# A gated top-2 dispatch: without the early two-row store, the first group of 65 rows in five stores of 13

## The chip, the cores and the metric

One core of a Trainium2 chip runs the kernel. The metric is the device time in microseconds. The kernel before takes 239.43 us, the median of three runs (239.3 to 239.44).

## What is computed

For each of 16 x 1024 tokens the kernel takes a vector of 512 float32 numbers and 8 router logits. It finds the two largest probabilities of the softmax, normalises them to sum 1, and writes the vector twice, once scaled by each.

```python
probs = np.exp(router_logits - logits_max)
probs = probs / np.sum(probs, axis=-1, keepdims=True)
topk_indices = np.argsort(probs, axis=-1)[..., -k:]
topk_probs = np.take_along_axis(probs, topk_indices, axis=-1)
topk_probs = topk_probs / np.sum(topk_probs, axis=-1, keepdims=True)
x_expanded = x[:, :, np.newaxis, :].repeat(k, axis=2)
return (x_expanded * topk_probs[..., np.newaxis]).astype(np.float32)
```

So `x`, 33.6 MB, is read once, and the output, 67.1 MB, is written once. The two weights depend only on the difference of the two largest logits: a sigmoid of it and a sigmoid of its negative.

## The kernel before

The 16384 tokens stand as 128 partitions of 128 rows. They are worked in two groups (`GROUPS`, L16), of 65 and of 63 rows on each partition. A "row" below is one row on all 128 partitions: 256 KB of `x`, or 512 KB of output, since each vector is written twice.

Two buffers in on-chip memory hold everything. `xs` has room for 65 rows of `x`, `osp` for 18 rows of output (L97, L98). A third, small tile, `WA`, holds the weights of all rows. The logits and the intermediate results of the weight calculation lie at the end of `osp` (L101, L102), so that no store can be written there before the weights are known.

For each group a loop issues the loads of `LOADS` on SyncE's queue (L112). After the first load of 6 rows it also issues two loads of logits (L105, L106), and VectorE and ScalarE work out the weights (L53 to L68). Then a second loop goes through `STORES` (L119). An entry names the number of rows, the home of the output, the number of rows that ScalarE multiplies rather than VectorE, and the queue that issues the store. The multiplication is one VectorE instruction for all its rows (L127), and two ScalarE instructions for each row of ScalarE's (L135). The store follows (L138).

The home of an output is either `osp` or `xs` itself. In `xs` a block of n output rows takes the place of 2n rows of `x` that have been multiplied already or are just being multiplied: output row i is written to rows a + 2i and a + 2i + 1, not ahead of the row that is read. The homes alternate, so that one can be filled while the other is being stored.

In the first group the loads have 6, 28 and 31 rows, and the stores 2, 16, 16, 16 and 15. The store of 2 rows needs only the first load; ScalarE's queue (q10 in the profile) issues it. All other transfers are issued by SyncE, in the order of the program, on one queue (q1): the three loads, four stores of group 0, two loads of group 1, four stores of group 1. A waiting instruction on SyncE holds up all that follow it there. The loads of group 1 go into the rows of `xs` that group 0's outputs occupy, and wait for those stores.

Of the kernel before, what the change touches and what calls it, by code (L numbers as in the profile page):

```python
# [1 line left out]

# [4 lines left out]

F32 = mybir.dt.float32
ALU = mybir.AluOpType
ACTF = mybir.ActivationFunctionType  # L10
P = 128
E = 8
D = 512


GROUPS = [65, 63]  # L16
M = sum(GROUPS)


LOADS = [[6, 28, 31], [32, 31]]  # L20


STORES = [
    [
        (2, ("osp", 0), 0, "ACT"),
        (16, ("osp", 2), 0, "SP"),
        (16, ("x", 2), 0, "SP"),
        (16, ("osp", 0), 4, "SP"),
        (15, ("x", 35), 0, "SP"),
    ],  # L30
    [
        (16, ("osp", 0), 1, "SP"),
        (16, ("x", 0), 0, "SP"),
        (16, ("osp", 0), 4, "SP"),
        (15, ("x", 33), 0, "SP"),
    ],
]
OSP = 18


def top2_weights(nc, scratch, logits, WA):

    used = [0]

    def cut(n):
        a = scratch[:, used[0] : used[0] + M * n].rearrange("p (m n) -> p m n", n=n)
        used[0] += M * n
        return a

    a, b = logits[:, :, 0:4], logits[:, :, 4:8]  # L50
    hi = cut(4)
    lo = b
    nc.vector.tensor_tensor(hi, a, b, op=ALU.max)  # L53
    nc.vector.tensor_tensor(lo, a, b, op=ALU.min)  # L54
    n = 4
    while n > 1:
        n //= 2
        a, b = hi[:, :, 0:n], hi[:, :, n : 2 * n]
        nhi, nlo, tmp = cut(n), cut(n), cut(n)
        nc.vector.tensor_tensor(tmp, lo[:, :, 0:n], lo[:, :, n : 2 * n], op=ALU.max)  # L60
        nc.vector.tensor_tensor(nlo, a, b, op=ALU.min)  # L61
        nc.vector.tensor_tensor(nlo, nlo, tmp, op=ALU.max)  # L62
        nc.vector.tensor_tensor(nhi, a, b, op=ALU.max)  # L63
        hi, lo = nhi, nlo
    dlt = cut(1)
    nc.vector.tensor_tensor(dlt, hi, lo, op=ALU.subtract)  # L66
    nc.scalar.activation(WA[:, :, 0], dlt[:, :, 0], ACTF.Sigmoid, scale=-1.0)  # L67
    nc.scalar.activation(WA[:, :, 1], dlt[:, :, 0], ACTF.Sigmoid, scale=1.0)  # L68


@with_exitstack
def kernel(
    ctx: ExitStack,
    tc: tile.TileContext,
    x: bass.AP,
    router_logits: bass.AP,
    k: bass.AP,
    out: bass.AP,
):
    nc = tc.nc  # L80
    N = x.shape[0] * x.shape[1]
    assert int(k) == 2 and router_logits.shape[-1] == E and x.shape[2] == D
    assert N == P * M
    xf = x.rearrange("b s d -> (b s) d")
    of = out.rearrange("b s k d -> (b s) k d")
    rf = router_logits.rearrange("b s e -> (b s) e")
    x_v, o_v, rl_v = [], [], []
    t0 = 0
    for n in GROUPS:
        t1 = t0 + P * n  # L90
        x_v.append(xf[t0:t1].rearrange("(p m) d -> p m d", p=P))
        o_v.append(of[t0:t1].rearrange("(p m) k d -> p m k d", p=P))
        rl_v.append(rf[t0:t1].rearrange("(p m) e -> p m e", p=P))
        t0 = t1

    pool = ctx.enter_context(tc.tile_pool(name="pool", bufs=1))
    xs = pool.tile([P, max(GROUPS), D], F32)  # L97
    osp = pool.tile([P, OSP, 2, D], F32)  # L98
    WA = pool.tile([P, M, 2], F32)

    logits = osp[:, OSP - 1].rearrange("p k d -> p (k d)").rearrange("p (m e) -> p m e", e=E)  # L101
    scratch = osp[:, OSP - 3 : OSP - 1].rearrange("p r k d -> p (r k d)")  # L102

    def load_logits():
        nc.sync.dma_start(logits[:, : GROUPS[0]], rl_v[0])  # L105
        nc.sync.dma_start(logits[:, GROUPS[0] :], rl_v[1])  # L106

    m0 = 0
    for g, G in enumerate(GROUPS):
        r = 0  # L110
        for n in LOADS[g]:
            nc.sync.dma_start(xs[:, r : r + n, :], x_v[g][:, r : r + n, :])  # L112
            if g == 0 and r < 6 <= r + n:
                load_logits()
                top2_weights(nc, scratch, logits, WA)
            r += n
        assert r == G
        r = 0
        for n, (home, a), by_act, queue in STORES[g]:  # L119
            if home == "x":  # L120
                og = xs[:, a : a + 2 * n, :].rearrange("p (r k) d -> p r k d", k=2)
            else:
                og = osp[:, a : a + n]
            v = n - by_act
            w = WA[:, m0 + r : m0 + r + n, :]
            if v:
                nc.vector.tensor_tensor(  # L127
                    og[:, :v],
                    xs[:, r : r + v, :].unsqueeze(2).to_broadcast([P, v, 2, D]),
                    w[:, :v].unsqueeze(3).to_broadcast([P, v, 2, D]),  # L130
                    op=ALU.mult,
                )
            for i in range(v, n):
                for c in range(2):
                    nc.scalar.activation(  # L135
                        og[:, i, c], xs[:, r + i, :], ACTF.Copy, scale=w[:, i, c : c + 1]
                    )
            {"SP": nc.sync, "ACT": nc.scalar}[queue].dma_start(o_v[g][:, r : r + n], og)  # L138
            r += n
        assert r == G  # L140
        m0 += G


# [1 line left out]
_INS = ['x', 'router_logits', 'k']  # L145
_OUTS = [((16, 1024, 2, 512), 'float32')]

_NUMBERS = {'k': 2}


# [26 lines left out]
```

## Time and profile before

| | |
|---|---|
| median of three runs | 239.43 us |
| the profiled execution's own time | 239.38 us |
| its span | 237.6 us |
| VectorE busy | 132.2 us |
| ScalarE busy | 13.2 us |
| moved, read and written | 34.08 MB and 67.11 MB |
| mean rate over the span | 426 GB/s |

The span runs from the first to the last event in the trace; the execution's own time holds a little more at both ends. A transfer's time to landing counts from its issue until its completion is signalled, and so includes the time that it stands in the queue behind others. In the tables of groups, a line gives the source line, the engine, the operation, the tiles with their shapes and the count, then the busy time with the mean of one in ns, then the idle time before it and what ended that. In the list of queues the three numbers are packets, megabytes, and busy time as a share of 16 engines over the stretch that was asked for. In the table of stretches a line gives the stretch, its length, the busy time and instructions of VectorE, ScalarE and GpSimd, TensorE's clock (here without meaning), the DMA share and GB/s. "SPq" and "ACTq" are the instructions by which SyncE and ScalarE issue transfers.

### The profile page before, as it was taken

What the parts mean: (1) busy time and instruction counts of PE and PEld (TensorE: products, weight loads), DVE (VectorE), ACT (ScalarE), POOL (GpSimd) and SP (SyncE); (2) the same over time, 40 slices, a digit from 0 to 9 for tenths busy, and PEclk for the clock granted to TensorE, in tenths of its full rate; (3) what the DMA queues carried; (4) which work ended last, traced back from release to release, by engine and by line L of the source; (5) the groups of instructions that cost most, each with busy time, mean ns of one, the idle gap of its engine ahead of it and who ended that gap; (6) DMA issues with size and microseconds to landing.
All of it is one profiled execution on the core that took longest, in us unless ns stands there. A gap on an engine that the chain in (4) does not pass through costs nothing.

```text
span 237.6 us, 124 instructions
## 1 busy us (share of the span) xinstructions
DVE 132.2 (56%) x20; ACT 13.2 (6%) x21; POOL 0.2 (0%) x4
## 2 busy tenths in 40 slices
DVE  0640599999289999000000009999956999920000
ACT  2000000000080000000000001000006100000000
POOL 0000000000000000000000000000000000000000
DMA  7979989898989989899998989898989989897995
GB/s 265 541 338 488 408 386 535 348 530 353 496 386 441 441 353 530 353 508 414 414 519 353 508 370 502 353 519 353 496 386 419 463 353 530 353 530 342 496 445 217
DMA packets 2304, 101.19 MB, mean 426 GB/s; under 512 B 256, under 2 KB 384, under 8 KB 512
## 3 DMA queue, kind: packets, MB, share of 16 engines
q1 hardware_dynamic: 2160, 100.14, 97.7%
q10 hardware_dynamic: 144, 1.05, 1.0%
HBM read 34.08 MB, written 67.11 MB: 426 GB/s over the span
## 4 chain that ended last, share of the span: by engine, by line
DMA 48%; DVE 39%; SPq 1%; issue 0%; DVEq 0%
DMA xs<-in_x_dram 30%; DVE osp L127 25%; DMA out_dram<-osp 19%; DVE xs L127 14%; SPq L105 0%; SPq L106 0%; SPq L112 0%; SPq L138 0%; DVEq L127 0%
## 5 line engine op out<-in xcount | busy, mean ns | idle before, releaser
L127 DVE TENSOR_TENSOR osp<-xs,WA 128x12288 f32<-128x12288 f32 (+3 forms) x5 | 61.6, 12318 | 68.7 <-DMA xs<-in_x_dram 58.4
L127 DVE TENSOR_TENSOR xs<-xs,WA 128x16384 f32<-128x16384 f32 (+1 forms) x4 | 66.8, 16692 | 0.3
L135 ACT ACTIVATE osp<-xs,WA 128x512 f32<-128x512 f32 x18 | 11.4, 709 | 161.3 <-DMA out_dram<-osp 90.0
L53 DVE TENSOR_TENSOR osp<-osp 128x512 f32<-128x512 f32 x1 | 0.7, 692 | 8.2 <-DMA osp<-in_router_logits_dram 8.2
L67 ACT ACT_TABLE_LOAD x1 | 1.3, 1283 | 0.7 <-PEq L158 0.7
L67 ACT ACTIVATE WA<-osp 128x128 f32<-128x128 f32 x1 | 0.3, 316 | 10.1 <-DVE osp L66 10.1
L54 DVE TENSOR_TENSOR osp<-osp 128x512 f32<-128x512 f32 x1 | 0.7, 693 | 0.0
L60 DVE TENSOR_TENSOR osp<-osp 128x256 f32<-128x256 f32 (+1 forms) x2 | 0.7, 352 | 0.0
L62 DVE TENSOR_TENSOR osp<-osp 128x256 f32<-128x256 f32 (+1 forms) x2 | 0.7, 352 | 0.0
L63 DVE TENSOR_TENSOR osp<-osp 128x256 f32<-128x256 f32 (+1 forms) x2 | 0.7, 352 | 0.0
L61 DVE TENSOR_TENSOR osp<-osp 128x256 f32<-128x256 f32 (+1 forms) x2 | 0.7, 351 | 0.0
L66 DVE TENSOR_TENSOR osp<-osp 128x128 f32<-128x128 f32 x1 | 0.3, 292 | 0.0
L68 ACT ACTIVATE WA<-osp 128x128 f32<-128x128 f32 x1 | 0.3, 298 | 0.0
L158 POOL MEMSET const-bfloat16-1.0<- 128x1 bf16 x1 | 0.1, 102 | 0.0
L158 POOL MEMSET const-uint8-127<- 128x1 uint8 x1 | 0.1, 102 | 0.0
L158 POOL MEMSET const-float32-0.0<- 128x1 f32 x1 | 0.1, 99 | 0.2 <-issue 0.2
L158 POOL MEMSET const-float32-1.0<- 128x1 f32 x1 | 0.1, 99 | 0.0
## 6 DMA issues: line engine op xcount, KB each, us to landing
xs<-in_x_dram SPq DMA_DIRECT2D x2, 7936.0 KB, 40.8
out_dram<-xs SPq DMA_DIRECT2D x2, 7680.0 KB, 27.5
xs<-in_x_dram SPq DMA_DIRECT2D x1, 7168.0 KB, 24.2
xs<-in_x_dram SPq DMA_DIRECT2D x1, 1536.0 KB, 6.0
out_dram<-osp ACTq DMA_DIRECT2D x1, 1024.0 KB, 24.5
osp<-in_router_logits_dram SPq DMA_DIRECT2D x1, 260.0 KB, 6.2
osp<-in_router_logits_dram SPq DMA_DIRECT2D x1, 252.0 KB, 6.4
out_dram<-osp SPq DMA_DIRECT2D x4, 23.9
```

The costliest lines, as they stand in the source:

```text
L53: nc.vector.tensor_tensor(hi, a, b, op=ALU.max)
L54: nc.vector.tensor_tensor(lo, a, b, op=ALU.min)
L60: nc.vector.tensor_tensor(tmp, lo[:, :, 0:n], lo[:, :, n : 2 * n], op=ALU.max)
L61: nc.vector.tensor_tensor(nlo, a, b, op=ALU.min)
L62: nc.vector.tensor_tensor(nlo, nlo, tmp, op=ALU.max)
L63: nc.vector.tensor_tensor(nhi, a, b, op=ALU.max)
L66: nc.vector.tensor_tensor(dlt, hi, lo, op=ALU.subtract)
L67: nc.scalar.activation(WA[:, :, 0], dlt[:, :, 0], ACTF.Sigmoid, scale=-1.0)
L68: nc.scalar.activation(WA[:, :, 1], dlt[:, :, 0], ACTF.Sigmoid, scale=1.0)
L127: nc.vector.tensor_tensor(og[:, :v], xs[:, r : r + v, :].unsqueeze(2).to_broadcast([P, v, 2, D]), w[:, :v].unsqueeze(3).to_broadcast([P, v ...
L135: nc.scalar.activation(og[:, i, c], xs[:, r + i, :], ACTF.Copy, scale=w[:, i, c : c + 1])
L158: nc = _bacc.Bacc("TRN2", target_bir_lowering=False, num_devices=1)
```

## The change

The early store of two rows is gone, and with it all use of ScalarE's queue. The first group's loads have 6, 31 and 28 rows, and its five stores 13 rows each, with homes `osp`, `xs`, `osp`, `xs`, `osp`; ScalarE multiplies three rows of the third and of the fifth. `osp` has 16 rows in place of 18, so that the logits and the intermediate results move down by two rows. Each load now names the place in `xs` where it puts its rows, and each store names its first row and that row's place; these places are the ones that the loops gave before. Group 1 keeps its loads, blocks and homes.

```diff
-LOADS = [[6, 28, 31], [32, 31]]
+LOADS = [[(6, 0), (31, 6), (28, 37)], [(32, 0), (31, 32)]]
 STORES = [
     [
-        (2, ("osp", 0), 0, "ACT"),
-        (16, ("osp", 2), 0, "SP"),
-        (16, ("x", 2), 0, "SP"),
-        (16, ("osp", 0), 4, "SP"),
-        (15, ("x", 35), 0, "SP"),
+        (0, 13, 0, ("osp", 0), 0, "SP"),
+        (13, 13, 13, ("x", 0), 0, "SP"),
+        (26, 13, 26, ("osp", 0), 3, "SP"),
+        (39, 13, 39, ("x", 26), 0, "SP"),
+        (52, 13, 52, ("osp", 0), 3, "SP"),
     ],
     [
-        (16, ("osp", 0), 1, "SP"),
-        (16, ("x", 0), 0, "SP"),
-        (16, ("osp", 0), 4, "SP"),
-        (15, ("x", 33), 0, "SP"),
+        (0, 16, 0, ("osp", 0), 1, "SP"),
+        (16, 16, 16, ("x", 0), 0, "SP"),
+        (32, 16, 32, ("osp", 0), 4, "SP"),
+        (48, 15, 48, ("x", 33), 0, "SP"),
     ],
 ]
-OSP = 18
+OSP = 16
...
-        for n in LOADS[g]:
-            nc.sync.dma_start(xs[:, r : r + n, :], x_v[g][:, r : r + n, :])
+        for n, s in LOADS[g]:
+            nc.sync.dma_start(xs[:, s : s + n, :], x_v[g][:, r : r + n, :])
...
-        for n, (home, a), by_act, queue in STORES[g]:
+        for r, n, s, (home, a), by_act, queue in STORES[g]:
...
-                    xs[:, r : r + v, :].unsqueeze(2).to_broadcast([P, v, 2, D]),
+                    xs[:, s : s + v, :].unsqueeze(2).to_broadcast([P, v, 2, D]),
...
-                        og[:, i, c], xs[:, r + i, :], ACTF.Copy, scale=w[:, i, c : c + 1]
+                        og[:, i, c], xs[:, s + i, :], ACTF.Copy, scale=w[:, i, c : c + 1]
```

More of the change, by code (lines that the diff above doesn't have):

```diff
@@ L117 @@
         assert r == G
-        r = 0
-        for n, (home, a), by_act, queue in STORES[g]:
+        for r, n, s, (home, a), by_act, queue in STORES[g]:
             if home == "x":
@@ L135 @@
                     nc.scalar.activation(
-                        og[:, i, c], xs[:, r + i, :], ACTF.Copy, scale=w[:, i, c : c + 1]
+                        og[:, i, c], xs[:, s + i, :], ACTF.Copy, scale=w[:, i, c : c + 1]
                     )
             {"SP": nc.sync, "ACT": nc.scalar}[queue].dma_start(o_v[g][:, r : r + n], og)
-            r += n
-        assert r == G
         m0 += G
```

## The prediction

> **What bounds the kernel now.** I read the page first, for the transfers' share of the span and the bytes.
>
> ```profile
> span 237.6 us, 124 instructions
> DVE 132.2 (56%) x20; ACT 13.2 (6%) x21; POOL 0.2 (0%) x4
> DMA  7979989898989989899998989898989989897995
> DMA packets 2304, 101.19 MB, mean 426 GB/s; under 512 B 256, under 2 KB 384, under 8 KB 512
> q1 hardware_dynamic: 2160, 100.14, 97.7%
> q10 hardware_dynamic: 144, 1.05, 1.0%
> ```
>
> VectorE works 56% of the time, the 16 DMA engines 98.7% (97.7 on SyncE's queue q1, 1.0 on ScalarE's q10). So the bytes set the time; compute matters only where it lets the queue run dry. Whether it ever does is the next question. I asked the busy table for five stretches, cut where transfers land; the last two columns are DMA share and GB/s.
>
> ```profile
> 7.90:20.70 12.80, 6.12 (x12) 0.51 (x2) 0.00 (x0) 1.00 1.02 440
> 20.70:26.40 5.70, 0.05 (x1) 0.00 (x0) 0.00 (x0) 1.00 1.00 408
> 26.40:46.50 20.10, 20.07 (x2) 0.00 (x0) 0.00 (x0) 1.00 1.00 432
> 46.50:122.90 76.40, 43.45 (x3) 5.01 (x8) 0.00 (x0) 1.00 1.00 432
> ```
>
> From 7.9 to 122.9 us the share is 1.00 throughout: no hole. One stretch, 20.7 to 26.4, is busy and yet slow: 408 GB/s against 432. Packets are booked when they end, so short stretches are coarse; landing times check it. Issue times come from the timeline, times to landing from the transfer list taken around each issue.
>
> ```profile
> 1.64 0.42 SPq L106 DMA_DIRECT2D osp<-in_router_logits_dram  x1
> osp<-in_router_logits_dram SPq DMA_DIRECT2D x1, 252.0 KB, 6.4
> 2.10 1.11 SPq L112 DMA_DIRECT2D xs<-in_x_dram  x2
> xs<-in_x_dram SPq DMA_DIRECT2D x1, 7168.0 KB, 24.2
> xs<-in_x_dram SPq DMA_DIRECT2D x1, 7936.0 KB, 43.8
> 14.95 0.37 ACTq L138 DMA_DIRECT2D out_dram<-osp  x1
> out_dram<-osp ACTq DMA_DIRECT2D x1, 1024.0 KB, 24.5
> 209.45 0.33 SPq L138 DMA_DIRECT2D out_dram<-xs  x1
> out_dram<-xs SPq DMA_DIRECT2D x1, 7680.0 KB, 27.3
> ```
>
> The second logits load lands at 1.64 + 6.4 = 8.04, the 28-row load at 26.3, the early store at 14.95 + 24.5 = 39.45, the 31-row load (second of the pair, issued at about 2.68) at 46.48, the last store at 236.75. Between 46.48 and 236.75 the queue moves 63 stored rows of group 0, 63 loaded and 63 stored of group 1: 33.03 + 16.52 + 33.03 = 82.58 MB in 190.27 us, **434.0 GB/s**. Between 8.04 and 46.48 it moves 59 loaded rows and the 2 early ones, 16.52 MB in 38.44 us; at 434.0 that is 38.05. The early stretch is thus 0.39 us slower than the rest, and the table puts some 0.32 of it (24/432 of 5.7 us) into the 5.7 us in which the early store first mixes with the loads. From 8.04 on, nothing but this 0.39 can be gained.
>
> **The change part by part.** Removed: the 2-row multiply and the early store with its own queue; their bytes move into larger transfers. Loads stay five, logit loads two, stores nine, the total 101.19 MB. ScalarE's issue of 0.37 us goes, worth nothing, since ScalarE then idles until 65.9. The 31-row load goes ahead of the 28-row one, and five stores of 13 rows take the place of 2, 16, 16, 16, 15. Each has to be issued before the transfer ahead of it in the queue is through. How long before? The shortest lead in this trace is at the first store of group 1:
>
> ```profile
> 122.89 0.34 SPq L112 DMA_DIRECT2D xs<-in_x_dram  x1
> xs<-in_x_dram SPq DMA_DIRECT2D x1, 7936.0 KB, 37.9
> 158.32 0.34 SPq L138 DMA_DIRECT2D out_dram<-osp  x1
> 158.32 21.80 DMA out_dram<-osp
> ```
>
> The load ahead lands at 122.89 + 37.9 = 160.79, the store at 180.12: 8.39 MB in 19.33 us, 434 GB/s, so nothing was lost with a lead of 160.79 - 158.32 = 2.47 us. Now the durations of the multiplications, by shape, and the two starts after a landing:
>
> ```profile
> L127 DVE TENSOR_TENSOR osp<-xs,WA 128x12288 f32<-128x12288 f32 x2 | 25.9, 12958 | 9.8 <-DMA out_dram<-osp 9.8
> L127 DVE TENSOR_TENSOR osp<-xs,WA 128x15360 f32<-128x15360 f32 x1 | 16.2, 16157 | 46.9 <-DMA xs<-in_x_dram 46.9
> L127 DVE TENSOR_TENSOR osp<-xs,WA 128x2048 f32<-128x2048 f32 x1 | 2.3, 2291 | 0.6 <-ACT WA L68 0.6
> 2.10 24.16 DMA xs<-in_x_dram
> 26.35 17.24 DVE osp L127
> 43.61 0.35 SPq L138 DMA_DIRECT2D out_dram<-osp  x1
> 43.61 22.22 DMA out_dram<-osp
> 65.95 12.97 DVE osp L127
> 65.94 5.01 ACT L135 ACTIVATE osp<-xs,WA 128x512 f32<-128x512 f32 x8 [53.34 <-DMA out_dram<-osp]
> ```
>
> Between 2048 and 12288 elements the slope is 1.042 ns per element, between 12288 and 15360 it is 1.041: 13 rows (13312) take 14.02 us, 10 rows (10240) 10.82. Six ScalarE rows take 3.8 (eight took 5.01), beside VectorE. VectorE begins 0.09 after a load's landing (2.10 + 24.16 = 26.26), 0.12 after a store's, SyncE issues 0.03 after VectorE's end. At 434.0 GB/s 31 loaded rows take 18.72 us, 28 rows 16.91, 13 stored rows 15.70. Hence, in the changed kernel:
>
> - 31-row load lands 8.04 + 18.72 = 26.76; VectorE 26.85 to 40.87; store 1 issued at 40.90. The 28-row load lands at 43.67: lead 2.77 us, above the proven 2.47. In the old order it was 46.48 - 43.61 = 2.87, also without a hole.
> - Store 2: VectorE ends 54.9, store 1 lands 59.37: lead 4.5.
> - Store 3 writes over the rows that store 1 reads: VectorE waits until 59.49, ends 70.31; store 2 lands 75.07: lead 4.8.
> - Store 4: ends 84.33, against 90.77: lead 6.4.
> - Store 5 waits for store 3: 90.89 to 101.71, against 106.47: lead 4.8. Behind it on SyncE stands group 1's first load, which needs rows that store 4 reads: issued at about 106.5, while store 5 runs until 122.17, lead 15.7. The 31-row load follows at once, where it waited before:
>
> ```profile
> SPq L112 <- DMA out_dram<-xs: 26.2, 1, 26.2
> ```
>
> That wait cost nothing either, with the other load in the queue. Group 1 is not touched: its loads land at 141.5 and 160.2, and its first store keeps its lead.
>
> So the queue stays full and the sum is bytes: 8.04 + (101.19 - 2.10) MB / 434.0 = 236.36 for the last landing, against 236.75. Behind it lie 0.85 us to the end of the span and 1.78 from the span to that execution's own time, 239.38: 236.36 + 0.85 + 1.78 = 238.99. The median of the runs is 239.43, 0.05 above the profiled one; **239.0** is my forecast in whole tenths.
>
> Does the 0.39 really belong to the early store? Its bounds: 0.06 at least (an estimate: q10 needed 1.0% of 237.6 = 2.38 to 2.5 us of the engines for 1.05 MB, which take 2.42 at 434.0), 0.39 at most. Against the full amount speaks that the second half of the early store, until 39.45, runs in a stretch at 432, so that mixing as such is not slow. For it speaks the place: the slow 5.7 us begin as its first packets land, and none of the other stretches shown has them. I take the upper end. The Trainium skill ("DMA: Bandwidth & Descriptors", Bandwidth) gives 341 GB/s for a 1 MB transfer against 425 for 16 MB; by it the early store's bytes would take 3.1 us, and moving them into large transfers would gain 0.66 rather than 0.06 (an estimate from that page). The trace disagrees: q10's 1.0% are about 2.4 us.
>
> **The rivals.**
>
> R1, nothing comes back. The slow stretch belongs to the first large loads or to chance and stays; only the smaller packets' 0.06 goes: 239.43 - 0.06 = 239.4. For it: the half of the early store that costs nothing. Against it: the slow stretch's place.
>
> R2, slower: the first store of 13 rows comes too late and the queue runs dry before it. Only the lead of store 1 has fallen near the limit (2.77, where 2.87 and 2.47 were enough), and the early store's 2.4 us of cover are gone from this stretch. The need is not known below 2.47. Above, the nearest row is the early store itself, alone in its ring:
>
> ```profile
> q10 hardware_dynamic: 2, 0.02, 0.8%
> q10 hardware_dynamic: 14, 0.11, 38.6%
> ```
>
> Between 15 and 20 us 2 of its packets ended, 14 more until 20.7: 5.1 us from issue to first data, though it had to take turns with the loads. Were that the need, the hole would be 5.1 - 2.8 = 2.3 us, and the time 241.3. It is slower than before from a hole of 0.39 on, that is a need of 3.16. The nearer row, same queue and same engine, is the lead of 2.47 with no hole; I take none. The Trainium skill (the same page, Latency and other measured facts) has a first byte after 0.6 us and HBM at 2 us under high load; added, as an estimate, these 2.6 us would leave store 1 almost no slack and still no hole.
>
> R3, faster than the sum: the early store cost idle time of the engines that shares do not show, by the page's rule 0.6 beside the slow stretch's 0.32, in all 0.9, 238.5. Against it: from 8.04 on only 0.39 lies above the steady rate, so the steady rate itself would have to rise.
>
> **How the numbers follow.** Forecast 50%, R1 28%, R2 14%, R3 8%. About 0.2% (0.48 us, so below 238.95 or above 239.91) is what a measurement of this kernel tells from no change. The forecast lies on the inner side of that line by a hair: with its own spread of 0.15 I give 20 of its 50 to faster, 30 to the same. R1 is the same, R3 faster. Of R2, a hole above 0.9 is slower (9), a smaller one the same (5). Faster 0.28, same 0.63, slower 0.09. The range reaches from half of R3's further gain, 238.7, to R1 with a small hole, 239.7; the forecast's own range is 238.8 to 239.2.
>
> **What would show it.** Right: DMA share 1.00 in every stretch from 8 to 122 us, no stretch near 408 GB/s before the first store, the 31-row load landing near 26.8, store 1 issued near 40.9 and landing near 59.4, group 1's first load landing near 141.5. R1: the 28-row load lands near 44.0 and group 1's first load near 141.9, with a slow stretch still there. R2: store 1 lands more than 15.8 us after the 28-row load. Wrong altogether: VectorE idle before stores 2, 4 or a last landing earlier than 236.0.

## The result, and the profile after

The changed kernel takes 240.73 us (median of five runs, 240.46 to 240.91) against 239.32 for the kernel before (five runs, 239.22 to 239.44). The ratio is 1.0057, 95% interval 1.0042 to 1.0072: slower by 1.4 us, where 0.4 less had been forecast. The profiled execution took 240.46; its page begins like this:

```profile
span 238.7 us, 129 instructions
DMA  7999899999999999999998989898989898999994
DMA packets 2304, 101.19 MB, mean 424 GB/s; under 512 B 256, under 2 KB 384, under 8 KB 512
q1 hardware_dynamic: 2304, 101.19, 98.4%
```

The bytes are the same, the engines look as busy as before, and the span is 1.1 us longer. Where it goes is seen in the chain of waits (start, duration, what):

```profile
2.10 24.68 DMA xs<-in_x_dram
26.90 14.04 DVE osp L128
40.95 18.49 DMA out_dram<-osp
59.47 10.84 DVE osp L128
84.44 22.07 DMA out_dram<-xs
106.52 36.55 DMA xs<-in_x_dram
143.20 16.17 DVE osp L128
159.43 21.72 DMA out_dram<-osp
```

In the kernel before, the same load stands in the chain as

```profile
95.58 46.42 DMA xs<-in_x_dram
```

and lands at 142.00.

Until 106.5 us the forecast's own table is met to 0.1 us: the 31-row load lands at 26.78 (26.76 forecast), store 1 is issued at 40.95 (40.90) and lands at 59.44 (59.37), store 4 lands at 106.51 (106.47). Then group 1's first load lands at 143.07, where 141.5 was forecast. The list of transfers around store 5 and the loads shows it in steps:

```profile
out_dram<-osp SPq DMA_DIRECT2D x1, 6656.0 KB, 21.1
xs<-in_x_dram SPq DMA_DIRECT2D x1, 7936.0 KB, 54.9
out_dram<-xs SPq DMA_DIRECT2D x1, 7680.0 KB, 27.4
```

The first line is store 5, the second the second load of group 1, the third the last store of all. Store 5, issued at 101.74, lands at 122.84, 16.3 us behind store 4 rather than 15.7. The first load lands 20.2 us behind it rather than 19.3. The second load (issued at 106.91) lands at 161.8, the last store at 210.49 + 27.4 = 237.9, 1.15 later than before. So the whole loss lies in **the crossing from the last store of group 0 to the loads of group 1**.

In the trace's records of single packets, every one of the 16 last packets of store 5 is longer than the 1.966 us that the others of its size take, by 0.18 to 0.77 us, 0.37 on the mean. The slowest engine then pauses for 0.82 us before its first load packet, at 123.32. A load has landed when the slowest engine is through: of the 16 signals for the first load, one from each engine, the last comes 0.87 us behind the one before it. So the first store of group 1 is issued at 159.43 rather than 158.32; 14 engines stand idle before it for 0.15 to 0.54 us. The slowest engine does not: from 123.32 to its end at 237.52 its packets follow each other without a gap. Its delay alone sets the end, and the idle time of the others costs nothing here.

For all kernels below I summed, packet by packet, what the large packets took beyond the usual shortest time of their size (the fifth percentile), as a mean over the 16 engines ("slow packets", in us). It counts no pauses, and each row comes from one profiled execution.

```text
kernel            16-115 us   115-135 us   after 135   median of runs
before               0.37        0.05         0.03        239.3
changed              0.03        0.40         0.22        240.7
late_second          0.03        0.48         0.20        240.8
load_26_37           0.08        0.52         1.05        241.8
early_back           0.47        0.22         0.03        239.9
before_late_load     0.28        0.13         0.01        239.3
last15               0.08        0.81         0.20        240.6
early_13             0.65        0.16         0.02        239.9
loads_26_26_11       0.05        0.40         0.79        241.9
four_16              0.15        1.03         0.37        241.3
before_sp            1.15        0.01         0.04        240.1
first_act            0.83        0.21         0.01        240.1
tiny_act             0.03        0.75         0.18        240.4
lead_g1              0.03        0.31         0.85        241.7
third_act            0.03        0.45         0.22        240.5
ring_mix             1.15        0.06         0.02        240.4
logits_act           0.31        0.87         0.00        243.6
early_1              0.05        0.73         0.01        239.6
before_lead          0.23        0.18         0.68        240.2
late_loads           0.07        0.33         0.02        239.6
```

### The profile page after: what moved, and what is told of

It reads as the page before. It is cut to its first block, busy times and chain, and to the rows that moved or that the text cites. A ratio compares the mean times of both kernels' runs of the same rounds, so it can differ in the third digit from the quotient of the medians.

```text
span 238.7 us, 129 instructions
## 1 busy us (share of the span) xinstructions
DVE 130.1 (54%) x20; ACT 15.7 (7%) x25; POOL 0.2 (0%) x4
## 4 chain that ended last, share of the span: by engine, by line
DMA 52%; DVE 35%; SPq 1%; issue 0%; DVEq 0%
DMA xs<-in_x_dram 26%; DVE osp L128 23%; DMA out_dram<-osp 17%; DVE xs L128 13%; DMA out_dram<-xs 9%; SPq L107 0%; SPq L108 0%; SPq L114 0%; DVEq L128 0%; SPq L139 0%
## 5 line engine op out<-in xcount | busy, mean ns | idle before, releaser
L128 DVE TENSOR_TENSOR osp<-xs,WA 128x10240 f32<-128x10240 f32 (+3 forms) x5 | 64.8, 12959 | 71.9 <-DMA xs<-in_x_dram 56.4
L128 DVE TENSOR_TENSOR xs<-xs,WA 128x13312 f32<-128x13312 f32 (+2 forms) x4 | 61.4, 15359 | 0.3
L136 ACT ACTIVATE osp<-xs,WA 128x512 f32<-128x512 f32 x22 | 13.9, 709 | 159.8 <-DMA out_dram<-osp 111.3
## 6 DMA issues: line engine op xcount, KB each, us to landing
out_dram<-xs SPq DMA_DIRECT2D x1, 7680.0 KB, 27.4
```

Of the source, the lines that this page charges most:

```text
L128: nc.vector.tensor_tensor(og[:, :v], xs[:, s : s + v, :].unsqueeze(2).to_broadcast([P, v, 2, D]), w[:, :v].unsqueeze(3).to_broadcast([P, v ...
L136: nc.scalar.activation(og[:, i, c], xs[:, s + i, :], ACTF.Copy, scale=w[:, i, c : c + 1])
```

## The experiments

Each kernel was timed in rounds beside the kernel before, which took 239.22 to 239.29 us in all of them.

### First: the two loads, their lead, the early store

Four theories of the slow crossing. A: two loads stand in the queue behind store 5, where the kernel before had one. B: the first load is issued at 106.5, too shortly ahead, where before it was 95.6. C: it comes from the early store's absence. D: the delay itself is small, and the late first store of group 1 makes the loss.

**late_second**, on the changed kernel; the load waits for GpSimd:

```diff
+            if g == 1 and r == 32:
+                nc.gpsimd.memset(osp[:, 12, 1, 511:512], 0.0)
+                nc.gpsimd.tensor_copy(xs[:, s, 0:1], osp[:, 12, 1, 511:512])
```

> The changed kernel, with group 1's second load held back until store 5 has landed (about 122 us), as the kernel before issued it; in the changed kernel both loads of group 1 are issued at 106.5. Theory A (the crossing from store 5 to the loads is slow because two loads stand in the queue behind it): the crossing is quick again, the first load of group 1 lands near 141.6 rather than 143.1, the time is 239.1 to 239.4. Theory B (the first load is issued too shortly ahead, 106.5 rather than 95.6) and theory C (the early store's absence, or the 13-row stores as such): no difference, 240.4 to 240.9.

240.78 us. The second load was issued at about 123.6, and the crossing was as slow as ever (0.48). A falls.

**before_late_load**, on the kernel before, the same two lines with `r == 0` and `xs[:, 0, 0:1]`, so that they wait for store 3:

> The kernel before, with group 1's first load held back until store 3 of SyncE has landed (104.6 rather than 95.6 us); the second load still waits for the last store's landing. Theory B (an issue shortly ahead of the crossing slows it): the first load lands 1 us or more later than 142.0, the time is 240.2 or more. Theories A, C and D: no difference, 239.2 to 239.5.

239.25 us, the load issued at 104.95. B falls.

**early_back**, on the changed kernel, `OSP = 18` and:

```diff
-        (0, 13, 0, ("osp", 0), 0, "SP"),
-        (13, 13, 13, ("x", 0), 0, "SP"),
-        (26, 13, 26, ("osp", 0), 3, "SP"),
-        (39, 13, 39, ("x", 26), 0, "SP"),
-        (52, 13, 52, ("osp", 0), 3, "SP"),
+        (0, 2, 0, ("osp", 0), 0, "ACT"),
+        (2, 13, 2, ("osp", 2), 0, "SP"),
+        (15, 13, 15, ("x", 0), 0, "SP"),
+        (28, 13, 28, ("osp", 2), 3, "SP"),
+        (41, 13, 41, ("x", 26), 0, "SP"),
+        (54, 11, 54, ("osp", 2), 2, "SP"),
```

> The changed kernel with the early store of 2 rows back on ScalarE's queue, and five stores of 13, 13, 13, 13, 11 rows behind it; osp has 18 rows again. Theory C (the early store's absence costs the time): 239.2 to 239.5. Theories A, B and D: the crossing from the last store of group 0 to group 1's loads stays as it is, 240.3 to 240.9, and the early store's stretch costs up to 0.4 more.

239.89 us: between the two expectations, 0.8 better than the changed kernel. With the early store the crossing at 120 us costs 0.22 rather than 0.40, and no engine falls far behind. C holds in part.

**load_26_37**, on the changed kernel:

```diff
-LOADS = [[(6, 0), (31, 6), (28, 37)], [(32, 0), (31, 32)]]
+LOADS = [[(6, 0), (31, 6), (28, 37)], [(26, 0), (37, 26)]]
```

> The changed kernel with group 1's loads of 26 and 37 rows rather than 32 and 31. The first needs only the rows of store 2 and is issued right behind store 5, near 102.1, and the first store of group 1 has a lead of about 6 us rather than 2.5. Theory D (the crossing delays one load's landing by 1.5 us, and the loss is that the first store of group 1 then comes too late): the hole is gone, 239.2 to 239.6. If the loss is time of the DMA engines themselves at the crossing, 240.2 to 240.7. Theory A expects a slow crossing here too, as the second load is issued at 106.5.

241.8 us (240.28 to 242.19), worse than both. Group 1's second store needs rows of the 37-row load, which I had overlooked; it was issued at 180.39, so late that most engines stood idle for about 1 us. But the larger surprise was elsewhere: the last packets of the 37-row load, ahead of a store that had been issued at 155.51, were slow by 0.87 us on the mean. The lead was meant to help there.

### Second: the size and the home of the last store

S: the crossing is slow where the last store's packets are smaller than the load's. H: where they come from `osp` rather than `xs`. E: where there was no early store.

**last15**: the fourth and fifth store of the changed kernel become

```diff
-        (39, 13, 39, ("x", 26), 0, "SP"),
-        (52, 13, 52, ("osp", 0), 3, "SP"),
+        (39, 11, 39, ("x", 26), 0, "SP"),
+        (50, 15, 50, ("osp", 0), 6, "SP"),
```

> The changed kernel with group 0's stores of 13, 13, 13, 11 and 15 rows rather than five of 13: the last store's packets have 60 KB as in the kernel before, and still come from osp, without the early store. Theory S (the crossing is slow where the last store's packets are smaller than those of the load behind it): a quick crossing, 239.1 to 239.6. Theories E (the early store, by its absence) and H (the last store comes from osp rather than xs): a slow one, the first load of group 1 lands near 143, 240.3 to 241.

**early_13**: as early_back, with stores of 2, 13, 12, 13, 12, 13 rows.

> The early store of 2 rows and then five of 13, 12, 13, 12, 13 rows: the last store has 13 rows from osp as in the changed kernel, but the early store is there. Theories S and H: slow crossing, 240.3 to 241. Theory E: as the kernel with the early store and 11 rows last, 239.7 to 240.0, or less.

**loads_26_26_11**:

```diff
-LOADS = [[(6, 0), (31, 6), (28, 37)], [(32, 0), (31, 32)]]
+LOADS = [[(6, 0), (31, 6), (28, 37)], [(26, 0), (26, 26), (11, 52)]]
```

> The changed kernel with group 1's loads of 26, 26 and 11 rows: the first load's packets have 52 KB, as the last store's, it is issued right behind store 5, and the first stores of group 1 have leads of 6 us and more. Theory S: a quick crossing, 239.0 to 239.5. Theories E and H: the packets at the crossing are slow by some 0.4 us on all engines and by 2 us on one; with the lead there is no hole behind them: 239.7 to 240.7.

**four_16** (the five stores of group 0 become four; of group 1 only the last changes):

```diff
-GROUPS = [65, 63]
+GROUPS = [64, 64]
...
+LOADS = [[(6, 0), (26, 6), (32, 32)], [(32, 0), (32, 32)]]
...
+        (0, 16, 0, ("osp", 0), 0, "SP"),
+        (16, 16, 16, ("x", 0), 0, "SP"),
+        (32, 16, 32, ("osp", 0), 4, "SP"),
+        (48, 16, 48, ("x", 32), 0, "SP"),
...
-        (48, 15, 48, ("x", 33), 0, "SP"),
+        (48, 16, 48, ("x", 32), 0, "SP"),
```

> No early store and no 13-row stores: groups of 64 and 64 rows, loads of 6, 26, 32 and 32, 32 rows, in both groups four stores of 16 rows with homes osp, xs, osp, xs; osp of 16 rows. The first store's lead is about 2 us. Theory E (the early store, by its absence): slow crossing from store 4 to group 1's loads, 240.2 to 241. Theories S (packets of equal size) and H (last store from xs): quick crossing, 239.0 to 239.5; if a lead of 2 us is too short, a hole before the first store adds up to 1 us.

240.64, 239.86, 241.91 and 241.26 us. The two kernels of 15-row and 16-row last stores without an early store are slow at the crossing (0.81 and 1.03), the one with an early store and 13 rows from `osp` is not (0.16): S and H fall, E holds. loads_26_26_11, slower than any theory had it, repeats load_26_37's surprise without its flaw: its first store was issued at 155.75 with a long lead, and the load packets ahead of it were slow by 0.79.

### Third: what about the early store does it?

Q: that a second queue is used. M: that stored packets mix with the loads. R: that 2 rows are stored by themselves.

**before_sp** and **first_act** change one word each, in the kernel before and in the changed one:

```diff
-        (2, ("osp", 0), 0, "ACT"),
+        (2, ("osp", 0), 0, "SP"),
```

```diff
-        (0, 13, 0, ("osp", 0), 0, "SP"),
+        (0, 13, 0, ("osp", 0), 0, "ACT"),
```

> The kernel before with its early store of 2 rows issued by SyncE, on the one queue behind the loads, rather than by ScalarE. Everything else is the same. Theory Q (a second queue in use makes the crossing from stores to loads cheap) and theory M (stored packets mixed among the loads do): slow crossing at 120 us, the first load of group 1 lands near 143, 240.2 to 241.2. Theory R (the 2 rows stored as a transfer of their own, on whatever queue): 239.0 to 239.5.

> The changed kernel with its first store of 13 rows issued by ScalarE, on its own queue, which so carries 6.8 MB from 41 us on. Theory Q: quick crossing, 239.0 to 239.8. Theory M: the store mixes with the last of the loads and with store 2, quick crossing too, with up to 0.4 us lost in the mix. Theory R: slow, 240.3 to 241.

**tiny_act** and **logits_act**, on the changed kernel:

```diff
+    extra = pool.tile([P, E], F32)
+    nc.scalar.dma_start(extra, rl_v[0][:, 0, :])
```

```diff
-        nc.sync.dma_start(logits[:, : GROUPS[0]], rl_v[0])
-        nc.sync.dma_start(logits[:, GROUPS[0] :], rl_v[1])
+        nc.scalar.dma_start(logits[:, : GROUPS[0]], rl_v[0])
+        nc.scalar.dma_start(logits[:, GROUPS[0] :], rl_v[1])
```

> The changed kernel with one more transfer, 32 bytes for each partition, loaded by ScalarE's queue into a tile of its own at the very start. Theory Q in its strict form (that the queue was used at all): quick crossing, 239.0 to 239.8. Theories M and R: no effect, 240.3 to 241.

> The changed kernel with both loads of logits issued by ScalarE, on its own queue beside the first loads: the second queue carries 16 packets on each engine among the loads, but no store. Theory Q: quick crossing, 239.0 to 239.8. Theory M, if it is stored packets that count: slow, 240.3 to 241; if any packets that set the engines apart count: quick.

240.13, 240.06, 240.36 and 243.64 us. tiny_act is slow at the crossing (0.75), so Q in its strict form falls. logits_act says little: the logits, taking turns with the large loads, landed only at 27.1 us, and everything behind them was late; its crossing was slow too (0.87).

before_sp was the key. The crossing at 120 us costs it nothing (0.01), as none of the theories but R expected, yet it is 0.9 us slower than the kernel before. The transfers around the 2-row store, by the list:

```profile
xs<-in_x_dram SPq DMA_DIRECT2D x1, 7936.0 KB, 42.4
out_dram<-osp SPq DMA_DIRECT2D x1, 1024.0 KB, 32.5
out_dram<-osp SPq DMA_DIRECT2D x1, 24.4
```

The store was issued at 15.04 and stood in the queue behind the load until 45. It landed at 47.54; the kernel before had moved the same bytes by 46.48. The last packets of the load ahead of it were slow by 1.12 us. R falls with the time, and a new reading comes up: a crossing is dear where the transfer behind it has stood ready for long.

### Fourth: the hole, a mix without loads, a store between two loads, one row

L: the slowest engine's own delay sets the end, whatever the others do. P: the cost of crossing is paid once, at whatever place comes first.

**lead_g1** (changed kernel) and later **before_lead** (kernel before) give ScalarE 6 rows of group 1's first store:

```diff
-        (0, 16, 0, ("osp", 0), 1, "SP"),
+        (0, 16, 0, ("osp", 0), 6, "SP"),
```

> The changed kernel with 6 rather than 1 row of group 1's first store multiplied by ScalarE: VectorE is done with it some 5 us earlier, and its lead grows from 2.5 to 7 us, so that a late landing of the load makes no hole before it. If the hole behind the late landing is the loss (theory D): 239.3 to 239.8. If the slowest DMA engine's own delay at the crossing is the loss, which sets the last landing whatever the other engines do (theory L): 240.3 to 240.9.

241.66 us (240.37 to 242.24): slower than the changed kernel. The profiled execution took 240.37, the least of the four, and its crossing left no engine far behind: the first load landed at 141.80, so that it had no late landing to make up for. The list of transfers, KB and us to landing, has its second load, issued at 106.92, and its first store of group 1, issued at 152.82:

```profile
xs<-in_x_dram SPq DMA_DIRECT2D x1, 7936.0 KB, 54.8
out_dram<-osp SPq DMA_DIRECT2D x1, 28.2
```

The load lands at 161.7, the store at 181.0. That is 19.9 us for the load behind the first one, where 18.7 is the steady rate: 1.2 us were lost in slow packets (0.85 on the mean, 1.41 on the slowest engine) ahead of the store that stood ready. So this run does not part D from L. The changed kernel's own packets do: its slowest engine works without a gap from the crossing to the end, which is L, and the hole of the others, which D blames, is not on its path.

**third_act** issues store 3 of the changed kernel on ScalarE's queue:

```diff
-        (26, 13, 26, ("osp", 0), 3, "SP"),
+        (26, 13, 26, ("osp", 0), 3, "ACT"),
```

> The changed kernel with the third store of group 0 issued by ScalarE, on its own queue: there it mixes with stores 2 and 4, but with no load. If anything that sets the engines out of step before the crossing makes it cheap (theory P): 239.2 to 239.8. If stored packets have to come among loaded ones (theory M): slow crossing, 240.3 to 241.

240.49 us (239.82 to 240.7), crossing 0.45: a second queue that mixes stores with stores does not help.

**ring_mix**: the kernel before, its 2-row store issued by SyncE between the loads of 28 and 31 rows. The body of the store loop becomes a function; its call is moved:

```diff
-        (2, ("osp", 0), 0, "ACT"),
+        (2, ("osp", 0), 0, "SP"),
...
             r += n
+            if g == 0 and r == 34:
+                store(g, 0, m0, STORES[g][0])
```

> The kernel before with its early store of 2 rows issued by SyncE between the loads of 28 and of 31 rows, so that the one queue carries it between two loads; the load of 31 rows is issued at about 15.4 us, long before its turn. Theory M (stored packets among the early loads make the later crossing cheap, on whatever queue): the crossing at 120 us is quick, and what the two turns at 26 us cost shows there; 239.2 to 240.2, less than 240.13 if the turns cost less than the one at 46 us did. Theory Q (a second queue): slow crossing at 120 us, 240.2 to 241.2.

240.39 us. The crossing at 120 us is free (0.06). The store, issued at 14.86, stood 11 us behind the 28-row load, whose last packets were slow by 1.14.

**early_1**, on the kernel before:

```diff
-        (2, ("osp", 0), 0, "ACT"),
-        (16, ("osp", 2), 0, "SP"),
-        (16, ("x", 2), 0, "SP"),
+        (1, ("osp", 0), 0, "ACT"),
+        (16, ("osp", 1), 0, "SP"),
+        (16, ("x", 1), 0, "SP"),
         (16, ("osp", 0), 4, "SP"),
-        (15, ("x", 35), 0, "SP"),
+        (16, ("x", 33), 0, "SP"),
```

> The kernel before with an early store of 1 row rather than 2, and 16, 16, 16, 16 rows behind it. Theory M with an amount (the more is mixed, the cheaper the crossing): between the two kernels, 239.5 to 240.5. If any early store will do, or the mix itself is what costs: 239.0 to 239.4.

239.58 us. One row mixed early costs 0.05 instead of 0.37, and the crossing at 120 us then costs 0.73 on the mean, more than in the changed kernel; yet the kernel is 1.15 us faster than that one. Its 16 engines are slow together: the last one signals the first load 0.21 us behind the middle of the 16, where it was 1.42 us in the changed kernel.

### Fifth: is it the standing ready?

W: a crossing from loads to stores, or back, costs up to 1 us where the transfer behind it has stood ready for more than a packet's time.

> The kernel before with 6 rather than 1 row of group 1's first store multiplied by ScalarE, the edit that made the changed kernel slower (lead_g1): the store stands ready 7 us, three packets, ahead of its turn, rather than 2.5. Theory W (a crossing from loads to stores, or back, costs up to 1 us where the transfer behind it has stood ready for more than a packet's time): the last packets of the second load are stretched, 239.9 to 240.6. Theory P (the cost of the crossings is paid once, and the early store's mixing has paid it): 239.1 to 239.4.

240.16 us: one number, in a kernel that had "paid" early, makes it 0.9 us slower. In its list of transfers the second load is issued at about 122.64, the store at 152.88:

```profile
xs<-in_x_dram SPq DMA_DIRECT2D x1, 7936.0 KB, 39.0
out_dram<-osp SPq DMA_DIRECT2D x1, 28.1
```

The load lands at 161.64 rather than 160.79, the store at 180.98 rather than 180.12, and the kernel ends that much later. P as a strict rule falls.

**late_loads**, on the changed kernel, ahead of group 1's loads, an extra multiplication over rows that are stored already; its result is overwritten by the load:

```diff
+        if g == 1:
+            nc.vector.tensor_tensor(xs[:, 8:32], xs[:, 8:32], xs[:, 8:32], op=ALU.mult)
```

> The changed kernel with group 1's loads issued only at about 119.5 us rather than 106.5, 2 us ahead of the end of store 5: VectorE, idle there, does one more multiplication of 24 rows that have been stored already, and the loads wait for it. Theory W: no load stands ready in time to stretch store 5's last packets, the crossing is quick, the first load lands near 141.6 and the time is 238.8 to 239.4, or up to 0.5 more if the loads come too late and leave a hole. Theory P: the crossing costs the same, 240.2 to 240.9.

239.58 us, 1.15 less than the changed kernel, by doing more work and issuing the loads 13 us later. Seven of ten runs lie at 239.38 to 239.73, three at 241.08 to 241.37; what the three had is open. The chain of the profiled execution (239.48):

```profile
84.55 22.11 DMA out_dram<-xs
106.74 12.97 DVE xs L114
119.73 22.35 DMA xs<-in_x_dram
142.20 16.17 DVE osp L130
158.43 21.75 DMA out_dram<-osp
```

The load, issued at 119.73, lands at 142.08 rather than 143.07, and no packet of store 5 is slow; the first packets of the load are, by 0.33. One doubt stays: VectorE works between 106.7 and 119.7 here, where it is idle in the changed kernel.

For crossings from loads to stores on SyncE's queue the runs give a clean scale. The lead is the landing of the load less the issue of the store; the cost is the mean of slow packets just ahead:

```text
kernel, place               lead us    slow packets us
early_1, group 0              1.9          0.00
before, group 1               2.5          0.01
changed, group 0              2.8          0.01
early_back, group 0           4.4          0.21
early_13, group 0             4.8          0.43
load_26_37, group 1           7.4          0.87
loads_26_26_11, group 1       7.7          0.79
before_lead, group 1          8.8          0.68
lead_g1, group 1              8.9          0.85
ring_mix, 2-row store        11.3          1.14
before_sp, 2-row store       30.0          1.12
```

All other crossings of this kind in which the store had a lead, of 2.0 to 3.9 us, cost 0.06 us or less.

No version beat the kernel before: the nearest, before_late_load, took 239.25 beside its 239.28.

## Why the prediction was wrong

**What held.** The bound (DMA bytes at 434 GB/s), the durations of all multiplications, the leads of stores 1 to 5 and every landing until 106.5 us. The early store's slow stretch was gone, as the forecast had it: 0.37 us of slow packets between 16 and 115 us became 0.03. The view that was to show it, the table of stretches at the old cuts, is no use for that (last two columns, DMA share and GB/s, of the changed kernel):

```profile
7.90:20.70 12.80, 3.82 (x11) 0.52 (x2) 0.00 (x0) 1.00 0.91 397
20.70:26.40 5.70, 0.00 (x0) 0.00 (x0) 0.00 (x0) 1.00 1.19 517
26.40:46.50 20.10, 19.56 (x2) 0.00 (x0) 0.00 (x0) 1.00 0.93 404
```

By the packet records a packet is booked whole in the stretch in which it starts (not when it ends, as the prediction has it), and 16 of them start nearly together. In 20.7:26.4 three such batches start, two of 63,488 and one of 57,344 bytes, which take 2 x 2.342 + 2.116 = 6.80 us, 1.19 of 5.7. A stretch that just takes in or just misses such a batch of about 1 MB reads 517 or 397, while landings and single packets show a steady rate. The early 408 was confirmed by packets, not by that table. One more reading in the prediction is off, without bearing on the sum: its "six ScalarE rows" are six ScalarE instructions, that is three rows.

**The step that failed** stands in the part-by-part account: "Behind it on SyncE stands group 1's first load ... issued at about 106.5, while store 5 runs until 122.17, lead 15.7", and then "its loads land at 141.5 and 160.2". I costed the crossing from store to load at nothing, because in the kernel before it took nothing. The runs show that it is not free in itself, in two ways. The first is the mean: up to 135 us the slow packets come to 0.42 us before and 0.43 in the changed kernel, so the crossing took back what the early store's absence gained. The second is the slowest engine. Half of the 16 engines have signalled the first load of group 1 by 141.70 us before and by 141.66 in the changed kernel; the last one follows 0.30 us later before, and 1.42 us later in the changed kernel. These 1.1 us are the loss against the kernel before.

The other kernels bear both out. In ten of the eleven kernels whose slow packets before 115 us came to 0.15 or less, the changed one among them, the crossing cost 0.31 to 1.03 us on the mean of the engines. The eleventh is late_loads, where the 0.33 lie in the load's own first packets. The kernel before had it for nothing in company with its early store, and I had put down the 0.37 us that the early store costs as pure loss. The slowest engine parts the kernels more clearly than the mean. In the profiled executions of eight kernels without an early store (the changed one, late_second, load_26_37, last15, loads_26_26_11, four_16, tiny_act, third_act) it signals the first load 1.02 to 1.59 us behind the middle of the 16; in the eight with an early store, on either queue, and in first_act, 0.21 to 0.50. The other three are lead_g1 (0.17), logits_act (0.32) and late_loads (0.55).

**The lead.** "Above the proven 2.47" was right as a lower bound; that a larger lead is at worst harmless was assumed throughout and is wrong. A store that stands ready 9 us ahead costs 0.7 to 0.9 us, shown by one number in before_lead. The holes give the lower bound more sharply: in load_26_37 the late store was issued at 180.39 into a queue run dry, and its first packets on 14 engines started 0.84 to 0.99 us later by the packet records. The Trainium skill ("DMA: Bandwidth & Descriptors", Rules for kernel authors) advises to issue a DMA early, so that its fixed cost is overlapped. These runs agree up to about 3.9 us of lead, where a crossing cost 0.06 us at most, and disagree from 4.4 us on: on a queue that is always full, a store issued 5.4 us earlier (152.88 rather than 158.32) made the kernel 0.9 us slower.

**The rivals.** R1 and R3 fell: the slow stretch did not stay, and nothing beyond it was gained. R2 had the sign, and the wrong place: store 1 landed 15.7 us behind the 28-row load (issued at 2.69, 41.0 us to landing), so there was no hole. The hole that did come, before group 1's first store, follows from the late load and lies on the engines that were not the slowest. The forecast's estimate of 2.6 us to a first byte, from the Trainium skill ("DMA: Bandwidth & Descriptors", Latency and other measured facts), is above the 0.84 to 0.99 us from issue to first packet measured here.

**What stays open.** Why the load behind the last store of group 0, ready for 16 us or more in either case, crosses almost for nothing in the kernel before, before_sp and ring_mix, and dearly in the changed kernel; and why one engine falls behind there without an early store, and hardly with one. That it goes with the early store's absence is shown by putting such a store back (early_back, early_13: 0.45 and 0.42 us in place of 1.42); by what means is open. For the mean, the common factor over the runs is that slow packets have occurred earlier, among the first loads (0.23 us or more before 115 us: 0.01 to 0.22 at the crossing, with logits_act, late from the start, as the exception at 0.31 and 0.87); before_lead shows that this does not cover a later crossing from loads to stores. The spread of the engines' packet starts at 110 us does not tell the kernels apart: 0.43 us in the kernel before, 0.42 in the changed one. The records do not name the engines, so whether it is always the same one that falls behind is open, and so is why it pauses for 0.8 us.

## What to carry to other kernels

On a saturated DMA queue, look at each turn from stores to loads and back, by landing times, and not only at holes: busy engines can be slow for a microsecond there. Ask of each landing how far the last engine is behind the others, since it sets the landing; a mean over the engines hides it. Issue the transfer behind a turn little more than one packet's time ahead, about 2 to 4 us here, rather than as early as possible; for turns from loads to stores this is shown, for turns from stores to loads it helped in one kernel. A transfer that costs a little where it stands may be saving more elsewhere, so before it is removed, its kernel's other turns should be measured without it.

## What the runs showed of the hardware

Packets ahead of a turn are stretched by up to 1.4 us each in ring_mix (57,344 bytes in 3.55 us rather than 2.12), and in the records the engine counts as busy all that time. A queue that has run dry takes 0.84 to 0.99 us from a store's issue to its first packets (load_26_37). An engine's delay is not shared out: the slowest of 16 sets the landing, and in the changed kernel the engine that fell behind at 122.5 us ended its last store at 237.52, 0.7 us behind the next.
